# A Strassen pair in a hybrid decoder trunk: the seventh product accumulates in the fifth's PSUM bank, and VectorE instead of GpSimd forms the weight sums

## The chip, the cores and the metric

One NeuronCore of a Trainium2 chip runs the whole program. The metric is the device time of one execution in microseconds (us). Engines: TensorE (PE, with its weight loads as PEld), VectorE (DVE), ScalarE (ACT), GpSimd (POOL), and SyncE (SP), which here only issues DMAs. Each engine works through its own queue in order.

## The reference

The reference is a decoder trunk of two layers over 1024 tokens of width 1024, all in float32. What matters of it:

```
for l in range(DEPTH):                       # DEPTH = 2
    h = rms_norm(x, norm1_w[l]) * (1 + sc1) + sh1
    x = x + g1 * hybrid_mixer(h, w_in[l], w_out[l], ...)
    h = rms_norm(x, norm2_w[l]) * (1 + sc2) + sh2
    x = x + g2 * conv_ffn(h, w_gate[l], w_val[l], conv_w[l], conv_b[l], w_down[l])
return rms_norm(x, final_norm_w)
```

The mixer projects h with one matrix `w_in` into eight groups of 512 columns, runs four retention heads (with a rotary turn of q and k) and four gated-recurrence heads (HGRN2) over them, multiplies by gates and projects back. The FFN forms `silu(conv(h @ w_gate)) * (h @ w_val)` with 2816 columns, then multiplies by `w_down`. The shifts, scales and gates (`sh1` and so on) come from a product with `ada_w`.

## The kernel before, in words

**Split products.** To keep float32 accuracy, every operand is split into a high part (rounded on ACT, line L329 for weights) and the remainder (DVE, L330). A product of a 128-row weight block with 512 tokens is three matmuls: high by high, high by low, low by high (L451, L452, L453). Each matmul has a 128x128 weight and 128x512 moving data.

**Pairs.** Most projections are done two at a time by `pair()`: two blocks of 128 output columns (`g` and `v`), each over all 1024 tokens, form a 2x2 block problem that a Strassen-Winograd scheme solves with seven products instead of eight. The activation side (`b11` to `b22`, and the sums `tops[1]` to `tops[3]`) is prepared once per stage. The weight side is prepared per pair: two DMAs bring `rg` and `rv` (two buffers in all, tag `raw`), four sums of 128x512 are formed on POOL (L472, L473, L474 after the first piece, L476 after the second), and `piece()` splits each of the seven weight blocks, in the order of the products, into six rotating buffers `whi`/`wlo`. `product()` runs 12 matmuls into one bank of a four-bank PSUM pool (tag `pr`). The results are combined by DVE additions that read one operand from SBUF and one from PSUM (`add`, L484); product 1 is copied to SBUF by ACT (L490). In the common order 1, 2, 4, 6, 7, 5, 3 a pair has seven such additions: one each after 2, 6 and 3, two after 7 (the second one uses the bank of product 4, kept until then), and two after 5. A pair with mode "late" (the q/k pair of head 0 in each layer) places product 4 later, because its operand `b12` is ready later; a pair with mode "plain" (the first FFN pair of each layer) uses another order.

**Stages.** In each layer the mixer has 14 pairs (three for f/q, three for the two values, four for q/k, four for the gates), the FFN has 20 (ft = 2 to 21, one of them "plain"). So the program has 68 pairs, 66 of them not "plain". In the mixer the pairs stand between the heads' own work, which generators (`chains`) emit in small steps: `step()` after each product lets every chain emit its next piece. The HGRN chain runs seven levels of small matmuls (L713, L723), each waiting for two DVE multiplications (L731, L732); before them DVE computes the forget gates (L673 to L677). The rotary turn uses a POOL multiplication (L617). In the FFN, `conv_act` runs per pair on ACT and DVE (L955 to L966) and stores through a DMA issued by POOL (L967).

**Other work on DVE.** The product with `ada_w` is done on DVE (L165, L167) in steps that `tick()` emits, one per `step()`. Its raw tiles (`aw`, two buffers) are brought by SP. During the FFN of layer 0 the steps for layer 1 are running; during the FFN of layer 1 there are none.

**Order.** The framework schedules at build time: each engine's order of instructions is fixed before the run, by priority and by a model of when operands are ready. Loads of weights, pieces, weight sums and additions stand in `hp()`, which moves them ahead of everything else by up to 4000 places.

Of the kernel before, what the change touches and what calls it, by code (L numbers as in the profile page):

```python
# [16 lines left out]
P = 128  # L17
# [23 lines left out]
def kernel(  # L41
# [8 lines left out]
    V, A, G, T = nc.vector, nc.scalar, nc.gpsimd, nc.tensor  # L50
# [8 lines left out]
    def hp():  # L59
        return tc.high_priority(offset=ahead[0])  # L60
# [14 lines left out]
    def pr_ps(name):  # L75
        return psum.tile([P, HALF], F32, tag="pr", name=name)
# [249 lines left out]
    def piece(src, n, nm):  # L326
        hi = stg.tile([P, HALF], F32R, tag="whi", bufs=NW, name=f"whi{nm}")
        lo = stg.tile([P, HALF], F32R, tag="wlo", bufs=NW, name=f"wlo{nm}")
        A.activation(hi[:, 0:n], src, AF.Copy)  # L329
        V.tensor_tensor(out=lo[:, 0:n], in0=src, in1=hi[:, 0:n], op=ALU.subtract)  # L330
        return [(hi[:, i:i + P], lo[:, i:i + P]) for i in range(0, n, P)]

    def load_raw(src, n, nm, early=None):
        raw = stg.tile([P, S], F32, tag="raw", bufs=2, name=f"raw{nm}")
        dst = raw[:, 0:n * P].rearrange("p (a b) -> p a b", a=n)
        if early:
            early.dma_start(out=dst, in_=src)
        else:
            with hp(), after_last():
                nc.sync.dma_start(out=dst, in_=src)  # L340
        return raw

    def stage(src, n, nm, early=None):
        raw = load_raw(src, n, nm, early)
        w = []
        with hp():
            for i in range(0, n, 4):
                m = min(4, n - i)
                w += piece(raw[:, i * P:(i + m) * P], m * P, f"{nm}_{i}")
        return w  # L350

    def w_src(w, l, n0, k0=0, n=KT):
        return w[l, k0 * P:(k0 + n) * P, n0:n0 + P].rearrange("(k p) n -> p k n", p=P)
# [23 lines left out]
    def need(n):  # L377
        for _ in range(100):
            if len(zfree) >= n:
                return  # L380
            step()
        raise RuntimeError(f"{len(zfree)} of {n} tiles free")

    def step():
        tick()
        for ch in list(chains):
            ch[0] -= 1
            if ch[0] <= 0:
                ch[0] = next(ch[1], 0)
                if ch[0] == 0:  # L390
                    chains.remove(ch)

    def unit(w, l, n0, nm, wt=None):
        wt = wt or wcols(w, l, n0, nm)
        pss = []
        for half in range(2):
            pss.append(pr_ps(f"u{nm}_{half}"))
            gemm_half(pss[-1], wt, half, range(KT))
            step()
        return pss  # L400
# [41 lines left out]
    def last_operand():  # L442
        for k in range(4):
            split(b12, k, xs[4 + k].t[:, 0:HALF])
            xs[4 + k].free()

    def product(w, b, nm):
        ps = pr_ps(nm)
        for k in range(4):
            (wh, wl), rh, rl = w[k], b[0][:, k, :], b[1][:, k, :]  # L450
            T.matmul(ps, wh, rh, start=k == 0, stop=False)  # L451
            T.matmul(ps, wh, rl, start=False, stop=False)  # L452
            T.matmul(ps, wl, rh, start=False, stop=k == 3)  # L453
        return ps


    ORDERS = {"": (1, 2, 4, 6, 7, 5, 3), "late": (1, 2, 6, 7, 4, 5, 3), "plain": (1, 2, 3, 6, 7, 4, 5)}

    def pair(src_g, src_v, nm, mode=""):
        rg = load_raw(src_g, KT, nm + "g")  # L460
        rv = load_raw(src_v, KT, nm + "v")
        a11, a12, a21, a22 = rg[:, 0:HALF], rg[:, HALF:S], rv[:, 0:HALF], rv[:, HALF:S]
        s1 = stg.tile([P, HALF], F32, tag="s1", bufs=2, name=f"s1{nm}")
        order = ORDERS[mode]
        src = {1: a11, 2: a12, 3: a12, 4: a22, 5: s1, 6: a11, 7: a21}
        right = {1: b11, 2: b21, 3: b22, 4: b12, 5: tops[1], 6: tops[2], 7: tops[3]}
        p = {}
        with hp():
            for i in order:
                p[i] = piece(src[i], HALF, f"{nm}{i}")  # L470
                if i == 1:
                    G.tensor_add(s1, a21, a22)  # L472
                    G.tensor_sub(a21, a11, a21)  # L473
                    G.tensor_sub(a11, s1, a11)  # L474
                elif i == 2:
                    G.tensor_sub(a12, a12, a11)  # L476
        need(2)
        g, v = Z(), Z()
        g0, g1, v0, v1 = g.t[:, 0:HALF], g.t[:, HALF:S], v.t[:, 0:HALF], v.t[:, HALF:S]
        done = {}  # L480

        def add(o, x, y):
            with hp():
                V.tensor_add(o, x, y)  # L484

        for i in order:
            m = done[i] = product(p[i], right[i], f"{nm}_{i}")
            if i == 1:
                with hp():
                    A.activation(v0, m, AF.Copy)  # L490
            elif i == 2:
                add(g0, v0, m)
            elif mode == "plain" and i == 3:
                with hp():
                    A.activation(g1, m, AF.Copy)
            elif i == 3:
                add(g1, g1, m)
            elif mode == "plain" and i == 6:
                add(v0, v0, m)
                with hp():  # L500
                    G.tensor_add(g1, g1, v0)
            elif i == 6:
                add(g1, v0, m)
            elif i == 7:
                add(v1, v0 if mode == "plain" else g1, m)
                if 4 in done:
                    add(v0, v1, done[4])
            elif i == 4 and 7 in done:
                add(v0, v1, m)
            elif i == 5:  # L510
                add(v1, v1, m)
                add(g1, g1, m)
            step()
        return g, v

# [235 lines left out]
    def value_chain(z, box, key, nm):  # L751
        yield 1
        transpose8(z.t, nm, copy_evac)
        yield 1
        box[key] = z

    def run(gen):
        chains.append([next(gen), gen])
# [3 lines left out]
    first, second = TokenNorm(0, 0, 0), TokenNorm(1, 0, 0)  # L762
# [84 lines left out]
    for l in range(DEPTH):  # L847
# [9 lines left out]
        def loose(src):  # L857
            z = Z()
            with hp():
                put(z, src, AF.Copy)  # L860
            return z

        for h in range(HEADS):
            box = {}
            if h:
                ahead[0] = HP
                fsrc, qsrc = pair(w_src(w_in, l, HF + h * P), w_src(w_in, l, HQ + h * P), f"h{l}_{h}")
            else:
                fsrc, qsrc = pre[0], pre[1]
            run(hgrn_chain(l, h, fsrc, qsrc, box))  # L870
            if h:
                a, b = pair(w_src(w_in, l, HV + h * P), w_src(w_in, l, RV + h * P), f"v{l}_{h}")
            else:
                a = loose(pre[2])
                b = loose(unit(w_in, l, RV, f"r{l}_0v", early))
                last_operand()
            if l == 0 and h == 0:
                ada_todo.extend((0, b) for b in range(4, 12))
            run(value_chain(a, box, "h", f"h{l}_{h}v"))
            run(value_chain(b, box, "r", f"r{l}_{h}v"))  # L880
            ahead[0] = HP
            q, k = pair(w_src(w_in, l, h * P), w_src(w_in, l, 512 + h * P), f"r{l}_{h}", "" if h else "late")
            run(ret_chain(l, h, q, k, box))
        m = {}
        order = []
# [32 lines left out]
        def wo_cols(n):  # L918
            w = wcols(w_out, l, n * P, f"wo{l}_{n}")
            return [w[i] for i in order]  # L920
# [3 lines left out]
        for n in range(5):  # L924
            load_xs(n + 1, xd[2 * l])
            w = wo_cols(n)
            for half in range(2):
                ps = pr_ps(f"wo{l}_{n}_{half}")
# [5 lines left out]
        first = TokenNorm(0, l, 1)  # L934
        hooks = {5: {5: first.rstd}, 6: {2: first.turn, 4: first.spread}}
        for half in range(2):
            for n in range(5, KT):
                ps = pr_ps(f"wo{l}_{n}_{half}")
# [34 lines left out]
        for ft in range(PLAIN):  # L973
            nm = f"f{l}_{ft}"
# [44 lines left out]
        for gi, n in enumerate(GROUPS[:-1]):  # L1019
            dw = lambda d: stage(w_src(w_down, l, d * P, starts[gi], n), n, f"dn{l}_{gi}_{d}")  # L1020
            if gi == 0:
                fill(0, 0, 2)
                w = dw(0)
                fill(0, 2, n)
                load_xs(0, xd[2 * l + 1])
            else:
                w = dw(0)
            fill(gi + 1, 0, fresh[gi + 1])
            for d in range(KT):
# [6 lines left out]
                w = dw(d + 1) if d + 1 < KT else None  # L1036
# [4 lines left out]
        nm = f"dn{l}_last"  # L1041
        more = l + 1 < DEPTH
        first, second = TokenNorm(0, l + 1, 0), TokenNorm(1, l + 1, 0)
# [23 lines left out]
        for half in range(2):  # L1067
            sl = slice(half * HALF, (half + 1) * HALF)
            for d in range(KT):
                w = stage(w_src(w_down, l, d * P, f0, GROUPS[-1]), GROUPS[-1], f"{nm}_{d}_{half}")  # L1070
                if half and d in hooks:
                    hooks[d]()
                ps = pr_ps(f"{nm}_{d}_{half}")
# [68 lines left out]
```

## Time and profile before

| | us |
|---|---|
| median of 3 runs | 2635.63 |
| lowest and highest | 2628.96, 2637.62 |
| the profiled execution | 2626.96 |
| its span, first to last instruction | 2625.2 |
| PE busy in the span | 2511.0 (96%) |
| DVE busy | 1873.7 (71%) |
| ACT busy | 998.0 (38%) |
| POOL busy | 603.2 (23%) |
| mean granted TensorE clock | 0.982 of 2.4 GHz |

All rows quoted below come from the profiled execution. Busy shares are averages over stages with different limits, so they are to be read stage by stage. Times inside the trace count from the start of the span. A busy PE is not PE at its peak: matmuls overlap, and one 128x512 matmul starts about 0.23 us after the one before it though each is shown as about 0.39 us long.

### The profile page before, as it was taken

To read this page: it belongs to the slowest core of one execution; us is meant where nothing else is said; L and a number is where in the kernel's file an instruction comes from. 1 tells how busy PE (TensorE), PEld (TensorE's weight loads), DVE (VectorE), ACT (ScalarE), POOL (GpSimd) and SP (SyncE) were. 2 spreads that over 40 slices of the span, in tenths; PEclk is the share of its full clock that TensorE was granted. 3 is DMA by queue.
4 is the path that set the end of the run, shared out by engine and by line. 5 is a ranking of instruction groups with operands and counts; after the bars stand their busy time and mean duration, and the time that the engine had idled before them with its cause. 6 is when DMAs were issued, how large, how long until landed. Compare 5 with 4: busy or idle time off the path is not lost.

```text
span 2625.2 us, 32721 instructions
## 1 busy us (share of the span) xinstructions
PE 2511.0 (96%) x12189; PEld 2069.1 (79%) x12189; DVE 1873.7 (71%) x2781; ACT 998.0 (38%) x1685; POOL 603.2 (23%) x480
## 2 busy tenths in 40 slices
PE   5889999999999999999998999999999999999998
PEld 4777877888788888788877788888877888887887
DVE  7987878865988989744378777777397777774435
ACT  4533433433533333412264334444154333342224
POOL 1512223120423322200013222222133332320000
PEclk7899999999999999999999999999999999999999
DMA  8222313553134444743231112225312222254313
GB/s 294 73 83 86 105 59 95 179 178 93 65 121 135 133 134 147 249 133 95 79 117 57 49 36 70 73 73 154 96 58 78 89 73 88 81 198 139 96 54 107
DMA packets 293920, 283.56 MB, mean 108 GB/s; under 512 B 10793, under 2 KB 240769, under 8 KB 293761
## 3 DMA queue, kind: packets, MB, share of 16 engines
q1 hardware_dynamic: 275904, 219.42, 27.2%
q0 software_dynamic: 17408, 61.88, 6.5%
q8 instruction: 96, 1.57, 0.3%
q14 instruction: 63, 0.52, 0.1%
q10 hardware_dynamic: 449, 0.17, 0.0%
HBM read 229.00 MB, written 52.43 MB: 107 GB/s over the span
## 4 chain that ended last, share of the span: by engine, by line
PE 69%; DVE 8%; issue 5%; DMA 2%; POOL 1%; ACT 1%; POOLq 0%; DVEq 0%; SPq 0%; ACTq 0%
PE f L451 8%; PE f L453 8%; PE f L452 8%; PE dn L529 4%; PE dn L528 4%; PE dn L527 4%; PE wo L527 2%; PE wo L528 2%; PE wo L529 2%; PE dn_last L527 2%; PE dn_last L529 2%; PE dn_last L528 2%; PE g L452 2%; PE g L451 2%; PE g L453 2%
## 5 line engine op out<-in xcount | busy, mean ns | idle before, releaser
L451 PE MATMUL f<-hhi,whif 128*128 128x512 f32 x640 | 253.2, 396 | 3.2 <-DVE z L484 3.2
L453 PE MATMUL f<-hhi,wlof 128*128 128x512 f32 x640 | 251.4, 393 | 0.0
L452 PE MATMUL f<-hlo,whif 128*128 128x512 f32 x640 | 250.0, 391 | 0.0
L484 DVE TENSOR_TENSOR z<-z,f 128x512 f32<-128x512 f32 x278 | 186.3, 682 | 76.9 <-PE f L453 66.8
L451 PE MATMUL f<-thi,whif 128*128 128x512 f32 x480 | 189.8, 395 | 4.4 <-ACT z L490 4.0
L453 PE MATMUL f<-thi,wlof 128*128 128x512 f32 x480 | 189.5, 395 | 0.0
L452 PE MATMUL f<-tlo,whif 128*128 128x512 f32 x480 | 189.5, 395 | 0.0
L529 PE MATMUL dn<-hhi,wlodn 128*128 128x512 f32 x384 | 151.7, 395 | 7.8 <-DVE wlodn L330 7.8
L527 PE MATMUL dn<-hhi,whidn 128*128 128x512 f32 x384 | 150.5, 392 | 0.0
L528 PE MATMUL dn<-hlo,whidn 128*128 128x512 f32 x384 | 150.3, 391 | 0.0
L167 DVE SCALAR_TENSOR_TENSOR ac<-aw,cact,ac 128x512 f32<-128x512 f32 x140 | 125.1, 894 | 30.5 <-DMA aw<-in_ada_w_dram 29.2
L451 PEld LDWEIGHTS f<-hhi,whif 128*128 128x128 f32 x640 | 120.6, 188 | 29.1 <-DVE z L484 2.6
L913 DVE SCALAR_TENSOR_TENSOR z<-dn,mod,z 128x512 f32<-128x512 f32 x64 | 48.0, 749 | 133.2 <-PE dn L529 133.2
L453 PEld LDWEIGHTS f<-hhi,wlof 128*128 128x128 f32 x640 | 120.6, 188 | 27.7
L452 PEld LDWEIGHTS f<-hlo,whif 128*128 128x128 f32 x640 | 120.6, 188 | 26.7
L916 POOL DMA_DIRECT2D xd<-z x48 | 26.0, 541 | 391.2 <-DVE z L913 363.2
L451 PEld LDWEIGHTS f<-thi,whif 128*128 128x128 f32 x480 | 90.6, 189 | 26.9 <-ACT z L490 4.9
L329 ACT ACTIVATE whidn<-rawdn 128x512 fp32r<-128x512 f32 x64 | 39.4, 627 | 184.6 <-PE dn L528 171.0
L453 PEld LDWEIGHTS f<-thi,wlof 128*128 128x128 f32 x480 | 90.5, 188 | 20.9
L452 PEld LDWEIGHTS f<-tlo,whif 128*128 128x128 f32 x480 | 90.3, 188 | 20.8
L713 PEld LDWEIGHTS lh<-z,z 128*128 128x128 f32 x640 | 78.3, 195 | 25.2 <-issue 21.3
L713 PE MATMUL lh<-z,z 128*128 128x64 f32 x640 | 78.5, 276 | 17.8 <-DVE z L732 17.7
(659 smaller groups left out, 6892.7 us busy)
## 6 DMA issues: line engine op xcount, KB each, us to landing
aw<-in_ada_w_dram SPq DMA_DIRECT2D x160, 256.0 KB, 3.0
acts<-z POOLq DMA_DIRECT2D x44, 512.0 KB, 3.0
z<-acts SPq DMA_DIRECT2D x44, 512.0 KB, 4.6
z<-xd POOLq DMA_DIRECT2D x32, 512.0 KB, 5.2
rawdn<-in_w_down_dram SPq DMA_DIRECT2D x32, 512.0 KB, 3.9
xd<-z POOLq DMA_DIRECT2D x52, 256.0 KB, 2.8
rawdn_last<-in_w_down_dram SPq DMA_DIRECT2D x32, 384.0 KB, 3.6
af<-in_ada_w_dram SPq DMA_DIRECT2D x16, 512.0 KB, 10.6
```

The costliest lines, as they stand in the source:

```text
L167: V.scalar_tensor_tensor(out=a, in0=raw, scalar=cact[:, k:k + 1], in1=a, op0=ALU.mult, op1=ALU.add)
L329: A.activation(hi[:, 0:n], src, AF.Copy)
L451: T.matmul(ps, wh, rh, start=k == 0, stop=False)
L452: T.matmul(ps, wh, rl, start=False, stop=False)
L453: T.matmul(ps, wl, rh, start=False, stop=k == 3)
L484: V.tensor_add(o, x, y)
L527: T.matmul(ps, a, rh, start=i == 0, stop=False)
L528: T.matmul(ps, a, rl, start=False, stop=False)
L529: T.matmul(ps, b, rh, start=False, stop=i == last)
L713: T.matmul(ps[:, c * 64:(c + 1) * 64].rearrange("p (b t) -> p b t", t=s), k.t[:, cs], qp.t[:, cs].rearrange("p (b t) -> p b t", t=s)[:, 1: ...
L913: V.scalar_tensor_tensor(out=x, in0=ps, scalar=mod[:, l * 48 + gate + d:][:, 0:1], in1=x, op0=ALU.mult, op1=ALU.add)
L916: nc.gpsimd.dma_start(out=dst[d, :, sl], in_=x)
```

## The change

Four edits to `pair()` and `product()`:

1. The four sums of weights move from POOL (`G`) to DVE (`V`).
2. The order of products becomes 1, 2, 6, 7, 5, 4, 3 for every pair that is not "plain"; the mode "late" goes.
3. Product 3 accumulates onto product 5 in the same PSUM bank, so its first matmul doesn't start a new sum.
4. The additions follow: after 7, `v0 = g1 + m7`; after 5, `v1 = v0 + m5`; after 4, `v0 = v0 + m4`; after 3, `g1 = g1 + (m5 + m3)`. That makes six additions, one fewer. The pair with mode "plain" keeps its additions and order; its sums move to DVE as well.

```diff
-    def product(w, b, nm):
-        ps = pr_ps(nm)
+    def product(w, b, nm, ps=None):
+        first = ps is None
+        ps = pr_ps(nm) if first else ps
...
-            T.matmul(ps, wh, rh, start=k == 0, stop=False)
+            T.matmul(ps, wh, rh, start=first and k == 0, stop=False, skip_group_check=True)
...
-    ORDERS = {"": (1, 2, 4, 6, 7, 5, 3), "late": (1, 2, 6, 7, 4, 5, 3), "plain": (1, 2, 3, 6, 7, 4, 5)}
+    ORDERS = {"": (1, 2, 6, 7, 5, 4, 3), "plain": (1, 2, 3, 6, 7, 4, 5)}
...
                 if i == 1:
-                    G.tensor_add(s1, a21, a22)
-                    G.tensor_sub(a21, a11, a21)
-                    G.tensor_sub(a11, s1, a11)
+                    V.tensor_add(s1, a21, a22)
+                    V.tensor_sub(a21, a11, a21)
+                    V.tensor_sub(a11, s1, a11)
                 elif i == 2:
-                    G.tensor_sub(a12, a12, a11)
+                    V.tensor_sub(a12, a12, a11)
...
-            m = done[i] = product(p[i], right[i], f"{nm}_{i}")
+            m = done[i] = product(p[i], right[i], f"{nm}_{i}", done[5] if i == 3 and not mode else None)
...
             elif i == 7:
-                add(v1, v0 if mode == "plain" else g1, m)
-                if 4 in done:
-                    add(v0, v1, done[4])
-            elif i == 4 and 7 in done:
-                add(v0, v1, m)
+                add(v1 if mode else v0, v0 if mode else g1, m)
+            elif i == 4:
+                add(v0, v1 if mode else v0, m)
             elif i == 5:
-                add(v1, v1, m)
-                add(g1, g1, m)
+                add(v1, v1 if mode else v0, m)
+                if mode:
+                    add(g1, g1, m)
...
-            q, k = pair(w_src(w_in, l, h * P), w_src(w_in, l, 512 + h * P), f"r{l}_{h}", "" if h else "late")
+            q, k = pair(w_src(w_in, l, h * P), w_src(w_in, l, 512 + h * P), f"r{l}_{h}")
```

## Rows read from the trace of the kernel before

**Rows 1.** Page, part 1: busy us, share of span, instructions of PE.

```profile
PE 2511.0 (96%) x12189; PEld 2069.1 (79%) x12189; DVE 1873.7 (71%) x2781; ACT 998.0 (38%) x1685; POOL 603.2 (23%) x480
```

**Rows 2.** Windows: length, busy PE, PEld, DVE, ACT, POOL, clock, DMA share, GB/s.

```profile
103.00:538.00 435.00, 398.62 (x2337) 337.51 (x2338) 355.28 (x597) 163.65 (x342) 114.23 (x73) 0.96 0.33 101
728.60:1086.60 358.00, 357.25 (x1587) 292.64 (x1586) 314.11 (x392) 125.95 (x181) 112.31 (x90) 1.00 0.45 141
1409.70:1811.90 402.20, 380.72 (x2260) 322.98 (x2260) 301.12 (x510) 157.62 (x329) 106.23 (x69) 0.99 0.22 68
2013.60:2304.10 290.50, 290.50 (x1262) 237.01 (x1261) 209.23 (x256) 106.62 (x151) 92.88 (x75) 1.00 0.26 83
```

**Rows 3.** Waits of PE: instruction, for what, us in total, times, longest.

```profile
PE lh L723 <- DVE z L732: 15.9, 7, 3.1
PE v L451 <- ACT z L490: 9.9, 2, 5.8
```

**Rows 4.** Windows of L472, then of L476 (first and last sum): POOL busy, count.

```profile
0.00:2625.20 2625.20, 103.47 (x68) 0.98 0.34 108
...
0.00:2625.20 2625.20, 104.01 (x68) 0.98 0.34 108
```

**Rows 5.** Windows of L330 (first two rows) and of L167 (third): DVE busy, count.

```profile
728.60:1086.60 358.00, 112.92 (x126) 1.00 0.45 141
2013.60:2304.10 290.50, 90.46 (x105) 1.00 0.26 83
...
728.60:1086.60 358.00, 62.59 (x63) 1.00 0.45 141
```

**Rows 6.** Timelines of DVE and SP, one FFN pair of layer 1: start, us, instruction.

```profile
2157.72 1.41 DVE L330 TENSOR_TENSOR wlof<-rawf_12v,whif 128x512 fp32r<-128x512 f32 x1
...
2160.52 0.68 DVE L330 TENSOR_TENSOR wlof<-rawf_12g,whif 128x512 fp32r<-128x512 f32 x1
2161.12 0.68 DVE L484 TENSOR_TENSOR z<-z,f 128x512 f32<-128x512 f32 x1
...
2163.89 0.69 DVE L330 TENSOR_TENSOR wlof<-rawf_12v,whif 128x512 fp32r<-128x512 f32 x1
...
2164.64 0.37 SPq L340 DMA_DIRECT2D rawf_13g<-in_w_gate_dram  x1
```

**Rows 7.** Timelines of PE and DVE, first and last full FFN pair of layer 0.

```profile
737.36 0.40 PE L453 MATMUL f<-thi,wlof 128*128 128x512 f32 x1
740.51 2.06 DVE L484 TENSOR_TENSOR z<-z,f 128x512 f32<-128x512 f32 x3
...
1074.65 0.39 PE L453 MATMUL f<-thi,wlof 128*128 128x512 f32 x1
...
1081.35 0.75 DVE L167 SCALAR_TENSOR_TENSOR ac<-aw,cact,ac 128x512 f32<-128x512 f32 x1 [1.75 <-DMA aw<-in_ada_w_dram]
1082.02 1.28 DVE L484 TENSOR_TENSOR z<-z,f 128x512 f32<-128x512 f32 x2
```

**Rows 8.** Waits of DVE's additions for PE, FFN of layer 0, then of layer 1.

```profile
DVE z L484 <- PE f L453: 2.8, 7, 0.6
...
DVE z L484 <- PE f L453: 55.6, 60, 1.5
```

**Rows 9.** Waits of ACT in the FFN of layer 0: a piece for a sum.

```profile
ACT whif L329 <- POOL rawf_16g L474: 4.0, 1, 4.0
```

**Rows 10.** Timelines of DVE and ACT around the value pair of head 1.

```profile
206.28 0.68 DVE L676 TENSOR_SCALAR z<-z 128x1024 f32<-128x1024 f32 x1
...
1491.41 1.79 DVE L676 TENSOR_SCALAR z<-z 128x1024 f32<-128x1024 f32 x1
...
1494.82 1.76 DVE L330 TENSOR_TENSOR wlor<-rawr_1g,whir 128x512 fp32r<-128x512 f32 x1
...
1499.60 0.60 ACT L490 ACTIVATE z<-v 128x512 f32<-128x512 f32 x1 [4.38 <-DVE z L677]
```

**Rows 11.** Window just after that wait, columns as in rows 2.

```profile
1500.00:1503.50 3.50, 3.25 (x8) 2.60 (x9) 3.50 (x6) 0.20 (x1) 0.00 (x0) 0.55 0.00 0
```

More of the change, by code (lines that the diff above doesn't have):

```diff
@@ L445, in last_operand @@
             xs[4 + k].free()
-    def product(w, b, nm):
-        ps = pr_ps(nm)
+    def product(w, b, nm, ps=None):
+        first = ps is None
+        ps = pr_ps(nm) if first else ps
         for k in range(4):
             (wh, wl), rh, rl = w[k], b[0][:, k, :], b[1][:, k, :]
-            T.matmul(ps, wh, rh, start=k == 0, stop=False)
-            T.matmul(ps, wh, rl, start=False, stop=False)
-            T.matmul(ps, wl, rh, start=False, stop=k == 3)
+            T.matmul(ps, wh, rh, start=first and k == 0, stop=False, skip_group_check=True)
+            T.matmul(ps, wh, rl, start=False, stop=False, skip_group_check=True)
+            T.matmul(ps, wl, rh, start=False, stop=k == 3, skip_group_check=True)
         return ps
-    ORDERS = {"": (1, 2, 4, 6, 7, 5, 3), "late": (1, 2, 6, 7, 4, 5, 3), "plain": (1, 2, 3, 6, 7, 4, 5)}
+    ORDERS = {"": (1, 2, 6, 7, 5, 4, 3), "plain": (1, 2, 3, 6, 7, 4, 5)}
     def pair(src_g, src_v, nm, mode=""):
```

## The prediction, made before the changed kernel was run

> **What bounds the kernel now.** I read the page's first part, then the windows by stage. PE is busy 2511.0 of 2625.2 us [rows 1], so all that any edit can win back is in the other 114 us and in stretches at the lower clock. The windows say where these lie [rows 2]. In the FFN stretch of layer 0, 18 pairs from 728.6 to 1086.6, PE is busy 357.25 of 358 us; in that of layer 1, 15 pairs, 290.50 of 290.50. One pair takes 290.5/15 = 19.37 us there, which is 84 matmuls at 0.23 us. In the two mixers PE is idle 435 - 398.6 = 36.4 and 402.2 - 380.7 = 21.5 us, 58 together; the granted clock is 0.96 and 0.99 there, some 4% of 435 and 1% of 402 or 21 us more. So a gain can come from the mixers alone, at most 58 + 21 = 79 us, and the FFN can only get worse.
>
> Then I read which wait ends last. In the mixers PE waits for DVE: for the level multiplications (L723 on L732, 15.9 us), and twice for the copy of product 1, 5.8 us the longest [rows 3]. So DVE decides, and the change adds to DVE. How full is it? 355 of 435, 314 of 358, 301 of 402 and 209 of 290.5 us [rows 2]: in the FFN of layer 0 a pair has 314/18 = 17.4 us of DVE in 19.9 us, in that of layer 1 13.9 in 19.4.
>
> **The sums on DVE.** The program has 68 x 4 = 272 of them. On DVE two instructions of 128x512 follow each other at 2161.12 - 2160.52 = 0.60 us [rows 6]; I take 0.60 for a sum, because the first of these two has two SBUF inputs as a sum has. That is 4 x 0.60 = 2.4 us a pair. The addition that falls away is worth 0.60, so 1.8 us a pair are added. Against that stands what POOL's sums cost DVE today. They take 103.47/68 = 1.52 us down to the last one's 104.01/68 = 1.53 [rows 4], and while they run, a DVE instruction with both inputs in SBUF is stretched: the remainder L330 takes 0.68 undisturbed and 1.76 beside POOL [rows 6, 10]. In the FFN of layer 0, L330 is 112.92/126 = 0.90 on the mean and L167 62.59/63 = 0.99; with 0.68 and, for L167, 0.75 [rows 7] undisturbed that is 126 x 0.22 + 63 x 0.24 = 43 us in 18 pairs, 2.4 a pair [rows 5]. In layer 1 it is 105 x (90.46/105 - 0.68) = 19 us in 15 pairs, 1.3 a pair [rows 5]. So per pair DVE gains 0.6 us in layer 0 (17.4 to 16.8 of 19.9) and loses 0.5 in layer 1 (13.9 to 14.4 of 19.4). In neither case does it reach PE's time: 0 us, hidden under the products. If the cover were gone, 68 x 1.8 = 122 us would be the price; if all stretching went and no sum found PE waiting, nothing would be lost at all.
>
> The Trainium skill, page "SBUF — State Buffer", section "Who interferes with whom", says that a VectorE instruction with two SBUF inputs contends with a GpSimd instruction that reads SBUF, and that the one that starts second waits until the first has finished. The trace agrees with its direction, 1.76 against 0.68 us [rows 6, 10]. It also speaks against the change: a moved sum has two SBUF inputs itself, and the 16 rotary products stay on POOL, so by the rule a sum that meets one is held as L330 is, 1.08 us, 16 x 1.08 = 17 us of DVE in the mixers at worst. In the FFN the rule leaves the sum as it is.
>
> **What is ready when.** ACT waits up to 4.0 us for POOL's third sum before it can split its block [rows 9]; with sums of 0.60 that wait goes, and ACT is free for its other work. A new wait comes for it: the first sum stands in DVE's in-order queue and needs the second raw block. On POOL it cost nothing to wait. Bounds: 0, if the scheduler has put it behind its DMA's landing, to about 2 us of idle DVE a pair; 16.8 + 2 = 18.8 still fits into 19.9, but additions behind it come later. I take 0.5. The order moves piece 4 (from `rv`) from third to sixth. Today the buffer of `rv` is free after product 7's piece, fifth (2163.89 + 0.69 = 2164.58), and SP issues the next load at once, 2164.64 [rows 6]; it will be one product of 2.75 us later at most. Nothing else is queued on SP behind it in layer 1; in layer 0 the `aw` loads are. Six weight buffers keep the pieces some five products, 13 us, ahead of PE, so this is 0 unless that lead is gone, when it costs its 2.75 us once a pair. POOL's queue loses four sums in front of each store of L967: 0 to a small gain, nobody waits for these stores.
>
> **The shared bank.** Product 3 may start only when `v1 = v0 + m5` has read the bank; between them lies product 4, 12 x 0.23 = 2.75 us. Before, PE hardly waited for any addition in the FFN, its idle time in layer 0's stretch being 358 - 357.25 = 0.75 us in all [rows 2]. In layer 1 the additions come at once: 60 of 105 found DVE idle and waiting for PE. In layer 0 only 7 of 126 did [rows 8], so there additions run late. In the first of its 18 pairs product 5 ends at 737.36 + 0.40 = 737.76, and its addition, the second of three from 740.51, ends about 741.8; product 3 would be due at 740.35: 1.4 us late. In the last it ends at 1082.02 + 0.68 = 1082.7, due 1077.6: 5.1 us late, part of it 1.75 us behind a load of `aw` [rows 7]. Over the 18 pairs these delays add up to some 19 us if nothing else changed. But a stalled PE lets DVE catch up, one addition no longer stands between those of 7 and 5, and DVE has 0.6 us more room a pair and no ACT piece held by POOL. Bounds 0 to 19; I take +4. Layer 1: 0. The accumulation itself costs PE nothing, 12 matmuls as before.
>
> **The mixers.** At the value pair of head 1 product 1's copy waits 4.38 us for the forget-gate chain on DVE, whose instructions are stretched to 1.79 and 1.76 from 0.68 by that pair's neighbour's sums [rows 10]. At least three to four are stretched by 1.1, 3.3 to 4.4 us, and two to four moved sums of 0.60 enter the same chain, 1.2 to 2.4: a gain of 1 to 3 us in each layer, say 4 together, with part of the half-speed window behind it (clock 0.55 over 3.5 us [rows 11]). Elsewhere a block of up to 2.4 us of sums with high priority can come ahead of a level's multiplications in 28 pairs, while POOL's stretching goes: -12 to +12, I take -1. Together -5.
>
> **The sum.** FFN layer 0 +4, FFN layer 1 0, mixers -5: -1 us. The profiled execution took 2626.96 us (span 2625.2), so 2626 there; it lies 8.7 below the median of the runs shown, 2635.63, so I forecast 2634.6 for the median.
>
> **Rivals.**
> - *Faster.* The mixers win more: the chains before L490 and L732 are as relieved as DVE's stretched instructions suggest, and the stalls that let the clock fall become too short for that. For it: PE waits for just these chains [rows 3, 10]. Against: the level waits of L723 lie beside the rotary product, which stays. Price: the 5.8 + 4.1 us at the two L490 waits to a half, 5 us, a quarter of the other 48 us of idle PE, 12, and 3 of the 21 us of clock, with nothing lost in the FFN: -20 us, or 2616.
> - *Slower.* The shared bank: in the FFN of layer 0 the addition of product 5 stays late, and product 3 waits. It decides from where that addition ends over 2.75 us after product 5. For it: 7 of 126 [rows 8] and the two pairs above, whose `aw` waits the change doesn't touch. Against: the relief. Price: 12 of the 19 us, since a stall lets DVE catch up, and 2 for the clock, the mixers unchanged: +14, or 2650.
> - *It does nothing that can be seen.* The sums are formed 13 us ahead of their use, wherever: within a few us of 2635.6. This is the forecast's own side.
>
> **Chances.** A measurement of this kernel can tell some 0.3%, 8 us, from no change. Forecast and third rival, within 8 us: 0.46. Faster, 2608 to 2627: 0.27. Slower, 2644 to 2660: 0.27. The likeliest case has its own range of 2628 to 2643; to leave no more than 2 in 10 out, the range is 2614 to 2654.
>
> **What the next profile would show.** POOL's busy time falls from 603 by about 400 us, DVE's from 1874 moves by no more than 50 either way. L330's mean in both FFN stretches falls to 0.68 to 0.70. The FFN of layer 1 keeps 19.37 us a pair. If the bank is the trouble, PE shows waits of L451 for L484 in the FFN of layer 0. If the sums wait for loads, DVE shows waits for `raw` tiles. I am wrong if the FFN of layer 1 gets slower, or if the mixers move by over 20 us.

## The result, and the profile after

The changed kernel takes 2619.74 us (median of 9 runs, 2616.74 to 2622.28), the kernel before 2633.05 beside it (9 runs, 2624.38 to 2637.62). The ratio is 0.9946, with a 95% interval of 0.9935 to 0.9958: 13 us or 0.5% faster, and more than the 0.3% that a measurement of this kernel can tell. The profiled execution took 2617.09 us, that of before 2626.96. The forecast was 2634.6 within 2614 to 2654, with "faster by over 0.3%" as one of the two less likely cases. So the range held, the middle lay 15 us too high.

In the changed kernel the lines behind L451 stand one lower: matmuls L452 to L454, additions L485, the copy of product 1 L491, the four sums L473, L474, L475, L477. Part 1 of its page, busy us, share and instructions by engine, answers to [rows 1]:

```profile
PE 2515.0 (96%) x12189; PEld 2070.9 (79%) x12189; DVE 1875.5 (72%) x2987; ACT 997.9 (38%) x1685; POOL 201.0 (8%) x208
```

POOL loses 402 us. DVE has 206 instructions more (272 sums come, 66 additions go) and yet only 1.8 us more of busy time: what it took over is paid by what is no longer stretched. That is read off in the windows of L330 and of L167 in the 18 FFN pairs of layer 0, and of L330 in 15 of layer 1 (length, DVE busy and count, clock, DMA share, GB/s), beside [rows 5]:

```profile
717.50:1077.00 359.50, 85.57 (x125) 0.99 0.44 141
2004.00:2294.00 290.00, 71.52 (x105) 1.00 0.25 81
...
717.50:1077.00 359.50, 47.11 (x63) 0.99 0.44 141
```

An L330 now takes 85.57/125 = 0.685 and 71.52/105 = 0.681 us (before 0.90 and 0.86), an L167 47.11/63 = 0.748 (before 0.99). The windows of all engines, in the columns of [rows 2], are these:

```profile
103.00:527.00 424.00, 398.76 (x2332) 338.04 (x2332) 355.74 (x636) 161.03 (x338) 31.88 (x20) 0.96 0.32 104
717.50:1077.00 359.50, 355.70 (x1571) 291.15 (x1570) 302.93 (x445) 129.36 (x183) 9.61 (x18) 0.99 0.44 141
2004.00:2294.00 290.00, 290.00 (x1259) 236.60 (x1258) 214.56 (x300) 106.17 (x150) 7.99 (x15) 1.00 0.25 81
```

In the first the same work has 11 us less, and PE's idle time went from 36.4 to 424 - 398.76 = 25.2 us at the same busy time. In the second PE is idle for 359.5 - 355.7 = 3.8 us, before for 0.75. Where the time went is seen best by the first matmul of each stage in the two traces:

| first matmul of | before, us | after, us | shift |
|---|---|---|---|
| the pairs, layer 0 | 99.71 | 99.32 | -0.4 |
| output projection, layer 0 | 554.51 | 543.07 | -11.5 |
| FFN pairs, layer 0 | 694.90 | 683.29 | -11.6 |
| down projection, layer 0 | 1099.33 | 1089.94 | -9.4 |
| the pairs, layer 1 | 1404.34 | 1395.32 | -9.0 |
| output projection, layer 1 | 1827.97 | 1814.83 | -13.1 |
| FFN pairs, layer 1 | 1968.85 | 1960.86 | -8.0 |
| down projection, layer 1 | 2358.92 | 2348.67 | -10.3 |
| end of the span | 2625.19 | 2615.32 | -9.9 |

The mixer of layer 0 gives 11 us, the FFN of layer 0 takes 2.2 back, the mixer of layer 1 gives 4 and the stage behind it takes 5 back, the FFN of layer 1 gives 2. The waits of PE say which chains were shortened (instruction, what for, us in total, times, longest; beside [rows 3]):

```profile
PE lh L713 <- DVE z L732: 10.6, 5, 4.9
PE v L452 <- ACT z L491: 7.7, 2, 4.3
PE f L452 <- DVE z L485: 6.8, 5, 3.8
...
PE lh L723 <- DVE z L732: 1.9, 1, 1.9
```

The level wait of L723 fell from 15.9 to 1.9 us, that of L713, which was not read for the forecast, from 17.7 to 10.6. The wait for product 1's copy fell only from 9.9 to 7.7. And PE's FFN products now wait 6.8 us for additions, before 3.2. 6.6 of it is in the FFN of layer 0, in four waits. Two of them, 3.80 and 1.30 us, are product 3's and stand between products 4 and 3 of a pair; the other two, 0.97 and 0.50 us, stand before other products and have nothing to do with the shared bank. PE's timeline at the longest, and DVE's below it (start, length, instruction, in brackets the idle time before and what ended it):

```profile
721.60 0.40 PE L454 MATMUL f<-hhi,wlof 128*128 128x512 f32 x1
725.79 0.80 PE L452 MATMUL f<-hhi,whif 128*128 128x512 f32 x1 [3.80 <-DVE z L485]
...
723.85 0.69 DVE L477 TENSOR_TENSOR rawf_4g<-rawf_4g 128x512 f32<-128x512 f32 x1
724.45 0.69 DVE L330 TENSOR_TENSOR wlof<-rawf_4g,whif 128x512 fp32r<-128x512 f32 x1
725.05 0.68 DVE L485 TENSOR_TENSOR z<-z,f 128x512 f32<-128x512 f32 x1
```

Product 3 has to wait until the addition at 725.05 has read product 5's bank; in front of it DVE's queue holds moved sums and the remainders that hang on them. The sums are not all of it: with the sums back on POOL (second experiment) the same product still waits 3.93 us. This is the wait that the prediction named, L452 for L485 in the new numbering.

### The profile page after: what moved, and what is told of

Its sections match the earlier page's. It is cut to its first block, busy times and chain, and to the rows that moved or that the text cites. A ratio compares the mean times of both kernels' runs of the same rounds, so it can differ in the third digit from the quotient of the medians.

```text
span 2615.3 us, 32201 instructions
## 1 busy us (share of the span) xinstructions
PE 2515.0 (96%) x12189; PEld 2070.9 (79%) x12189; DVE 1875.5 (72%) x2987; ACT 997.9 (38%) x1685; POOL 201.0 (8%) x208
## 4 chain that ended last, share of the span: by engine, by line
PE 77%; DVE 13%; DMA 4%; issue 3%; ACT 2%; POOL 0%; SPq 0%; ACTq 0%; DVEq 0%; POOLq 0%
PE f L452 9%; PE f L454 9%; PE f L453 9%; PE dn L529 5%; PE dn L528 4%; PE dn L527 4%; PE lh L713 3%; PE wo L527 2%; PE wo L528 2%; PE wo L529 2%; PE dn_last L527 2%; PE dn_last L529 2%; PE dn_last L528 2%; PE r L452 2%; PE r L454 2%
## 5 line engine op out<-in xcount | busy, mean ns | idle before, releaser
L452 PE MATMUL f<-hhi,whif 128*128 128x512 f32 x640 | 253.8, 397 | 6.8 <-DVE z L485 6.8
L454 PE MATMUL f<-hhi,wlof 128*128 128x512 f32 x640 | 251.6, 393 | 0.0
L485 DVE TENSOR_TENSOR z<-z,f 128x512 f32<-128x512 f32 x240 | 164.1, 685 | 111.4 <-PE f L454 99.3
L452 PE MATMUL f<-thi,whif 128*128 128x512 f32 x480 | 189.5, 395 | 0.2 <-ACT z L607 0.2
L454 PE MATMUL f<-thi,wlof 128*128 128x512 f32 x480 | 189.5, 395 | 0.0
L452 PEld LDWEIGHTS f<-hhi,whif 128*128 128x128 f32 x640 | 120.9, 189 | 33.6 <-DVE z L485 7.2
L454 PEld LDWEIGHTS f<-hhi,wlof 128*128 128x128 f32 x640 | 120.8, 189 | 27.8
L167 DVE SCALAR_TENSOR_TENSOR ac<-aw,cact,ac 128x512 f32<-128x512 f32 x140 | 105.7, 755 | 29.7 <-DMA aw<-in_ada_w_dram 28.3
L452 PEld LDWEIGHTS f<-thi,whif 128*128 128x128 f32 x480 | 90.5, 188 | 21.6 <-ACT z L607 0.6
L454 PEld LDWEIGHTS f<-thi,wlof 128*128 128x128 f32 x480 | 90.5, 188 | 20.9
L713 PEld LDWEIGHTS lh<-z,z 128*128 128x128 f32 x640 | 79.3, 198 | 18.3 <-issue 15.9
L529 PEld LDWEIGHTS dn<-hhi,wlodn 128*128 128x128 f32 x384 | 72.6, 189 | 23.5 <-DVE wlodn L330 7.7
L713 PE MATMUL lh<-z,z 128*128 128x64 f32 x640 | 79.9, 279 | 11.2 <-DVE z L732 10.6
```

Of the source, the lines that this page charges most:

```text
L167: V.scalar_tensor_tensor(out=a, in0=raw, scalar=cact[:, k:k + 1], in1=a, op0=ALU.mult, op1=ALU.add)
L452: T.matmul(ps, wh, rh, start=first and k == 0, stop=False, skip_group_check=True)
L454: T.matmul(ps, wl, rh, start=False, stop=k == 3, skip_group_check=True)
L529: T.matmul(ps, b, rh, start=False, stop=i == last)
L713: T.matmul(ps[:, c * 64:(c + 1) * 64].rearrange("p (b t) -> p b t", t=s), k.t[:, cs], qp.t[:, cs].rearrange("p (b t) -> p b t", t=s)[:, 1: ...
```

## The experiments

They were run in four groups, each beside the kernel before (medians 2632.44, 2633.68, 2635.0 and 2635.8 us). All ratios below are to that kernel, with their 95% intervals.

**The parts of the change.** First the kernel before with the four sums alone moved to DVE.

```diff
-                    G.tensor_add(s1, a21, a22)
+                    V.tensor_add(s1, a21, a22)
... (and so the other three sums)
```

> The kernel before with one edit: the four weight sums of each pair on VectorE; order of products, banks and additions as before. Theory A (the gain comes from VectorE no longer being stretched beside POOL's sums): 8 to 14 us faster than before, nearly all of it in the mixer of layer 0; the mean of L330 in both FFN stretches 0.68 to 0.70 us. Theory B (the gain comes from the new order, the shared bank and the addition saved): within 3 us of before. Theory C (the gain comes from the sums being ready earlier, so that ScalarE isn't held): 8 to 14 us faster, as A.

Measured: 2621.85 us, 0.9955 (0.9937 to 0.9973), 10.6 us faster. L330 falls as in the whole change. So the sums bring 11 of the 13 us, and the order, the shared bank and the saved addition, put together, are worth no more than the rest of 3, which is not told from zero. The total is as theories A and C had it, the place is not. The profiled execution, at 2625.98 us the slowest of the six, has 3.5 us less than before in the mixer of layer 0 (by first matmuls), but 3.7 more in that of layer 1, and the level waits of L723 and L713 fall only from 33.6 to 24.1 us. In which stages the 10.6 us lie is open.

Then the opposite: the whole change, but the four sums stay on POOL.

```diff
-                    V.tensor_add(s1, a21, a22)
+                    G.tensor_add(s1, a21, a22)
... (and so the other three sums)
```

> The changed kernel with the four weight sums back on POOL: new order, shared bank and six additions stay. Theory A: between 2 us faster and 6 us slower than before, and waits of the third product's first matmul for an addition in the FFN of layer 0, since additions run late there; L330 0.86 to 0.90 us. Theory B: 8 to 14 us faster than before. Theory C: as A, but the third product needs POOL's sums earlier, so up to 8 us slower.

Measured: 2670.91 us, 1.0139 (1.0117 to 1.0161), 38 us slower, far outside what was expected: alone, the order with the shared bank is a bad change. PE's longest list of waits now begins with the bank, all of it in the FFN of layer 0:

```profile
PE f L452 <- DVE z L485: 16.2, 14, 3.9
```

12 of these 14 waits, 15.0 us, are product 3's. In the mixers product 3 waits another 14.6 us for additions.

Next the change with product 3 in a bank of its own, and so with the seventh addition.

```diff
-            m = done[i] = product(p[i], right[i], f"{nm}_{i}", done[5] if i == 3 and not mode else None)
+            m = done[i] = product(p[i], right[i], f"{nm}_{i}", None)
...
-                if mode:
-                    add(g1, g1, m)
+                add(g1, g1, m)
```

> The changed kernel with product 3 in a bank of its own again, and so a seventh addition (g1 = g1 + m5); sums on VectorE and the new order stay. Theory A: within 3 us of the changed kernel; the waits of a first matmul for an addition in the FFN of layer 0 (3.8 us the longest) go, VectorE is busy 66 x 0.6 = 40 us more. Theory B: loses 5 us or more against the changed kernel.

Measured: 2613.40 us, 0.9924 (0.9904 to 0.9945), 19 us faster. PE's FFN products wait 1.9 us for additions, the longest 1.1. The saved addition is thus worth less than what the shared bank costs, by some 6 us (0.9946 against 0.9924; the two intervals overlap at their edges), where theory A had no difference and theory B a loss. The FFN of layer 0 takes 398.1 us by first matmuls, with the shared bank 406.7: there the bank costs 8.6 us. From the kernel with the sums alone moved this one differs by the order of products, which here gains some 8 us (0.9955 against 0.9924, again with overlapping edges).

To part order and bank, the last kernel with its sums on POOL, which is the new order alone:

```diff
-                    V.tensor_add(s1, a21, a22)
+                    G.tensor_add(s1, a21, a22)
... (and so the other three sums)
```

> The kernel before with the new order of products alone: sums on POOL, product 3 in a bank of its own, seven additions. It stands beside the run that has the new order and the shared bank with sums on POOL (38 us slower than before). Theory A (those 38 us are the shared bank's, whose release waits for additions that POOL's contention makes late): within 6 us of before, and no wait of PE for an addition in the FFN of layer 0 over 2 us. Rival D (they come from the order: piece 6, third now, needs POOL's third sum): 25 to 40 us slower than before, with PE or ScalarE waiting for pieces.

Measured: 2659.05 us, 1.0088 (1.0069 to 1.0106), 25 us slower. PE's FFN products wait 2.2 us for additions instead of 16.2, so of the 38 us of the run above about 13 belong to the bank and 25 to the order, the lower end of what rival D had. What the order does is seen in ACT: its splits wait for POOL's third sum (here L475), 237 us in 50 cases by these waits, while in the kernel before ACT waits 78 us for POOL's sums. One in the FFN of layer 1, ACT's timeline:

```profile
2108.10 0.63 ACT L329 ACTIVATE whif<-rawf_8g 128x512 fp32r<-128x512 f32 x1 [3.85 <-POOL rawf_8g L475]
```

In the old order the piece for product 4, which needs no sum, stood between the second piece and the one that needs the third sum; in the new one nothing does. The wait alone costs nothing where PE decides: from the first FFN matmul to the down projection's of layer 1 this kernel takes the same time as the one before. Its loss lies in the mixers and at the stages' ends. That ACT's wait for the third sum makes it there is argued, not shown: a kernel in which POOL forms no sums at all, further down, loses as much by this order.

**Contention or latency.** If the gain comes from sums that are sooner ready, POOL work that nobody waits for must be free; if it comes from DVE's stretched instructions, it must cost. So POOL was given additions back whose result nobody reads, in the changed kernel four per pair (`whole[1]` and `whole[2]` are the split blocks of the first two pieces):

```diff
                     V.tensor_sub(a11, s1, a11)
+                    for _ in range(3):
+                        G.tensor_add(junk, whole[1][0], whole[1][1])
                 elif i == 2:
                     V.tensor_sub(a12, a12, a11)
+                    G.tensor_add(junk, whole[2][0], whole[2][1])
```

> The changed kernel with POOL given four additions a pair of the same size that nobody reads, three after the first piece's split and one after the second's: VectorE's sums stay, but POOL reads SBUF beside VectorE as it did before. Theory A: L330 is stretched again to 0.85 us or more in the FFN stretches, and 8 us or more of the gain go, in the mixer of layer 0 above all. Theory B and theory C: within 3 us of the changed kernel, since order, banks and the time at which the sums are ready stay.

Measured: 2780.19 us, 1.0552 (1.0527 to 1.0576), 148 us slower, far more than was expected. The direction speaks for contention, the size says that the test was too coarse: each DVE instruction that overlaps an idle addition, taken against the median of its form elsewhere, adds up to 225 us of stretch, where the real sums in the kernel before make 137; and the shared bank and the idle work together let PE wait 51.7 us for additions. A smaller dose without the shared bank was therefore tried, two idle additions a pair in the kernel with product 3's own bank.

```diff
                     V.tensor_sub(a11, s1, a11)
+                    for _ in range(2):
+                        G.tensor_add(junk, whole[0], whole[1])
```

> Sums on VectorE, new order, product 3 in its own bank (that kernel took 2613 us), and two additions a pair on POOL that nobody reads, after the first piece's split; half of POOL's work before, and no shared bank. Theory A (contention): VectorE busy 80 to 120 us more, and 8 to 30 us slower than without the two additions. Theory C (only the time at which the sums are ready counts): within 4 us of 2613.

Measured: 2659.48 us, 1.0089 (1.0072 to 1.0106), 46 us above the same kernel without them (43 by the two ratios), more than the 30 that theory A had as its most. DVE and POOL in part 1 of its page:

```profile
PE 2528.2 (95%) x12189; PEld 2076.8 (78%) x12189; DVE 2002.3 (75%) x3053; ACT 990.3 (37%) x1685; POOL 413.3 (16%) x344
```

DVE has the same 3053 instructions as without them, and 2002.3 - 1909.2 = 93 us more of busy time. The idle additions share buffers with the real sums and pieces, but no wait in this trace ends with one of them. So POOL's arithmetic costs DVE's time by itself, and the kernel pays for part of it. Whether sums that are ready sooner bring something beside that is not shown by these two runs.

**The rest of POOL's arithmetic.** Then what POOL still computes should go too. The rotary multiplication L617 on DVE, in the kernel with product 3's own bank:

```diff
-        G.tensor_mul(sw.t, sw.t, sn.t)
+        V.tensor_mul(sw.t, sw.t, sn.t)
```

> Sums on VectorE, new order, product 3 in its own bank (2613 us), and the 16 rotary multiplications of 128x1024 on VectorE as well instead of POOL. Theory A: VectorE gets 16 x 1.2 = 19 us more work and loses some 30 us of stretching, level multiplications L731 and L732 fall to 0.68 us; 2 to 8 us faster than 2613, in both mixers. Rival: a rotary multiplication ahead of a level's multiplications in VectorE's queue holds PE, 2 to 8 us slower.

Measured: 2606.63 us, 0.9888 (0.9871 to 0.9906), 7 us better than without it, as theory A had it. But it is not in both mixers: by first matmuls that of layer 0 takes 14.1 us more than without (439.1 to 453.2), that of layer 1 18.5 less (425.4 to 406.9). Then also the sums of the activation side (L419, L431, L436, L438, L439) and the plain pair's two additions (L501 in the kernel before), which leaves POOL without arithmetic:

```diff
-                G.tensor_add(xs[k].t[:, HALF:S], b12[0][:, k, :], b12[1][:, k, :])
+                V.tensor_add(xs[k].t[:, HALF:S], b12[0][:, k, :], b12[1][:, k, :])
...
-            G.tensor_sub(h12, h22, h12)
+            V.tensor_sub(h12, h22, h12)
... (and so L436, L438, L439, L501)
```

> As the one with the rotary multiplications on VectorE, and also the sums of the activation side and the two additions of the plain pairs: POOL has no arithmetic left. Theory A: VectorE gets 38 x 0.6 = 23 us more work and loses some 35 us of stretching at the two stage boundaries of each layer; another 0 to 8 us faster. Rival: at these boundaries two engines shared the work, and one alone takes longer: 4 to 12 us slower than with the rotary multiplications alone.

Measured: 2596.99 us, 0.9850 (0.9829 to 0.9871), another 10 us, a little more than theory A's 8. With all of that moved, the old order and the new one with the shared bank were compared again:

```diff
-        G.tensor_mul(sw.t, sw.t, sn.t)
+        V.tensor_mul(sw.t, sw.t, sn.t)
... (and so every addition, subtraction and multiplication on G)
```

> The kernel before with all of POOL's arithmetic on VectorE; order of products, banks and additions as before. It stands beside the run with the new order, product 3 in its own bank and no arithmetic on POOL (2597 us). Theory A (contention is nearly all of it): within 5 us of 2597. Rival E (the order brings its own part, as the 8 us between the two kernels with the sums alone on VectorE suggest): 5 to 12 us slower than 2597.

> The changed kernel with all of POOL's arithmetic on VectorE; product 3 in the fifth's bank. Theory A (the shared bank costs only where additions run late, and they run late because of contention): within 4 us of 2597. Rival F (the wait for the addition costs whatever the contention, as additions also stand behind loads of the ada product): 4 to 8 us slower than 2597.

Measured: 2572.78 us, 0.9755 (0.9726 to 0.9785), and 2574.38 us, 0.9763 (0.9734 to 0.9792). None of the expectations held: both lie 23 to 24 us below 2597. The first is the kernel before with nothing but the engine changed, and by the two ratios it is some 50 us faster than the changed kernel; part 1 of its page:

```profile
PE 2502.9 (97%) x12189; PEld 2066.3 (80%) x12189; DVE 1883.9 (73%) x3111; ACT 1004.7 (39%) x1685; POOL 79.0 (3%) x150
```

330 instructions have moved to DVE and its busy time grew by 10 us. By first matmuls 15.8 and 15.6 us of the gain lie in the two mixers, 8.1 in the FFN of layer 0, 9.9 in the stage behind that and 6.0 ahead of the first pair. Two causes go together in it: POOL no longer stretches DVE's instructions, and what POOL computed is ready sooner. A rotary multiplication takes 2.71 us on POOL and 1.22 on DVE, and before, ACT waited 18.1 us for POOL's activation sums (L431), of which nothing is left. No run parts the two.

Between these two kernels no difference is left: PE waits for additions 1.9 us in all in the second. So where additions come in time, the shared bank shows no price.

The kernel without POOL arithmetic and with product 3's own bank is 23 us slower than the second of these, though it differs in that bank and one addition. It is also 24 us slower than the first, from which it differs by the order of products alone. With the sums alone moved that order gained 8 us, so what it is worth hangs on the rest of the kernel, and why stays open. Its trace shows more stretches at the lower clock in the mixer of layer 0; the two longest (columns as in [rows 2]):

```profile
144.40:161.50 17.10, 12.95 (x50) 11.75 (x50) 11.38 (x15) 2.71 (x3) 0.00 (x0) 0.50 0.05 15
202.40:212.70 10.30, 8.21 (x32) 7.27 (x31) 8.57 (x13) 1.75 (x4) 0.98 (x1) 0.50 0.13 52
```

To see whether the rotary products hurt there by crowding DVE, those of layer 0 were put back on POOL in this kernel:

```diff
-        V.tensor_mul(sw.t, sw.t, sn.t)
+        (V if l else G).tensor_mul(sw.t, sw.t, sn.t)
```

> As the kernel of 2597 us (new order, own bank), but layer 0's rotary multiplications stay on POOL. In that kernel the mixer of layer 0 lost 12 us against the one with the rotary multiplications on POOL, 17 us of it at half clock behind the level waits. If this is the rotary multiplications' place in VectorE's queue: 4 to 14 us faster than 2597. If it is a shift of the fixed order alone: within 4 us, or slower.

Measured: 2585.66 us, 0.9807 (0.9776 to 0.9837), 11 us faster, as expected of crowding. But the two kernels above have all rotary products on DVE and are faster still. Every one of these kernels also has another fixed order on each engine, and with it other stalls in the mixers; differences of up to some 25 us between kernels that differ in much else are not put down to one mechanism here.

Last, the sums alone on POOL, everything else on DVE, in the old order:

```diff
-                    V.tensor_add(s1, a21, a22)
+                    G.tensor_add(s1, a21, a22)
... (and so the other three sums)
```

> The kernel before with all of POOL's arithmetic on VectorE except the four weight sums of each pair (rotary multiplications, the sums of the activation side and two additions move). Moving the sums alone gave 11 us, moving all 62 us, both with the old order. If the parts add up: 45 to 55 us faster than before. If the sums' contention is what counts wherever they stand (theory A at its plainest, 272 of POOL's 326 arithmetic instructions): at most 20 us faster. In between, each part is worth more when the other has gone.

Measured: 2595.77 us, 0.9856 (0.9831 to 0.9881), between the two expectations. The other 58 instructions (POOL has 208 in the changed kernel and 150 without arithmetic; with the 272 sums that makes 330, not the 326 of the expectation) are so worth 40 us when they move first, while the 272 sums are worth 11 when they move first and 62 - 40 = 22 when they move last (27 by the ratios, over two groups). The sums stretch DVE by 137 us in the kernel before and 149 here, but of the 137 some 70 lie in the pairs of the two FFNs, where PE decides. The 58 stand in the mixers and at the stages' ends, where DVE does; they stretch it by some 65 us before, and some of them are waited for themselves.

## Why the prediction was right, and what was mis-sized

*What bounds the kernel.* Right for the mixers: most of the gain came from there. Not right for the FFN, which "can only get worse" by the forecast: the windows that were read began behind the plain pair of each layer. There PE waited, before the change, 2.0 us in each layer for the copy of product 1, and in layer 0 another 2.17 us for an addition (PE's waits, whole span, columns as in [rows 3]):

```profile
PE f L451 <- ACT z L490: 4.0, 2, 2.0
PE f L451 <- DVE z L484: 3.2, 3, 2.2
```

In the changed kernel the first of these is gone. The FFN of layer 1 gained 2 us by that; in layer 0 the gain is hidden by the bank (below).

*DVE's account.* Right to about a tenth. Per pair 302.93/18 = 16.8 us in layer 0 (forecast 16.8) and 214.56/15 = 14.3 in layer 1 (14.4); L330 and L167 as forecast; POOL -402 (-400). The step that took the stretch from the mean of L330 against its undisturbed length holds. The Trainium skill's page "SBUF — State Buffer", section "Who interferes with whom", says that a VectorE instruction with two SBUF inputs contends with a GpSimd instruction that reads SBUF; the trace agrees in kind, as two idle POOL additions a pair made DVE 93 us busier. What the prediction held against the change by it, sums held by the rotary products for up to 17 us, came to little: the stretch by L617, counted over all DVE instructions, went from some 30 to 34 us.

*The sums' wait for loads.* 0.5 us a pair was taken. DVE waits 22.1 us for `raw` pieces at L473, 0.3 a pair; but 0.5 of it in the FFN of layer 0, none in that of layer 1, and nearly all in the mixers, where DVE has no time to spare. The mean was near, the place was not looked at.

*The value pair of head 1.* A gain of 4 us was forecast, from its chain alone. It mostly did not come: the longest waits for product 1's copy went from 5.8 to 3.3 in layer 0 and from 4.1 to 4.3 in layer 1. DVE's timeline in layer 1, to be held against [rows 10], shows why:

```profile
1476.75 0.69 DVE L473 TENSOR_TENSOR s1r<-rawr_1v 128x512 f32<-128x512 f32 x1 [3.46 <-DMA rawr_1v<-in_w_in_dram]
...
1483.08 0.69 DVE L676 TENSOR_SCALAR z<-z 128x1024 f32<-128x1024 f32 x1
```

The stretch is gone, L676 takes 0.69 instead of 1.79. By this timeline what it gave went into the sums' wait of 3.46 us at the head of the same chain, and into the sums that stand inside it.

*The mixers elsewhere.* This is the mis-sized term: -1 was taken, between -12 and +12. Measured, both mixers give 11 + 4 = 15 us, and with the 2.2 us at the value pairs (9.9 to 7.7) some 13 of that lie elsewhere, 5 of them given back behind the mixer of layer 1. The level waits of L723 and L713 fell by 33.6 - 12.5 = 21 us; in their place others grew, as that of the retention scores for the rotary turn (L639 for L619, 0.2 to 7.0). The end of the bounds was near, the middle was wrong by this reading: the blocks of sums at high priority and the stretching were set off against each other as if alike. But the four sums add 2.4 us to a queue once a pair, while the stretch falls on the multiplications between two levels, for which PE stands waiting. Of the 112 level multiplications (L731, L732) 20 took over 0.8 us before and 4 after, and together they went from 101.0 to 85.1 us. The reading is not shown to the end: with the sums alone moved it is also 4 and 85.2 us, yet that trace keeps 24.1 us of level waits. How much of the 13 us is this relief and how much another fixed order of each engine is open. The "faster" rival named these relieved chains; its 20 us were too many, since the clock of the first window stayed at 0.96 and the waits behind the levels grew.

*The shared bank.* The place and the mechanism were right; that the stage came out near the term, +2.2 for +4, is luck. Against the kernel with product 3's own bank the bank costs 8.6 us in the FFN of layer 0 (398.1 to 406.7 by first matmuls), over twice the term: 5.1 us of waits of product 3, the longest 3.8, and a stretch at the lower clock behind that one (the stage's mean granted clock is 0.99 with it and 1.00 without). What hid this are 6.3 us that the same stage gains without the shared bank, 404.4 before to 398.1, which the forecast had at nothing. The reason for relief was right: 37 of some 108 additions (six a pair) now find DVE idle and waiting for PE, before 7 of 126 [rows 8]. The "slower" rival holds where that relief is taken away: with the sums left on POOL the FFN of layer 0 takes 423.8 us, and 405.3 with the same order and product 3's own bank, so the bank costs 18.5 there; 14 had been given, with 19 as the bound. So what decides on its price is how late the additions run, and that hangs on POOL.

*The order.* It was costed at nothing, for the buffer of `rv` alone. By itself it costs 25 us with the sums on POOL, gains some 8 with the sums alone on DVE, and costs 24 again with no arithmetic on POOL. That the third sum is needed one piece sooner fits the first of these figures and can't explain the last. In the change the sums are on DVE, so the total did not show it.

*The sum.* -1 was forecast, -10 measured between the two profiled executions (2626.96 to 2617.09): -15 in the mixers for -5, +2 for +4, and +3 for 0 in the rest, the +5 behind the mixer of layer 1 and the -2 in its FFN. The direction of each large term was right; that the total stayed within the range owes something to the bank's price, which took back part of what the mixers and the FFN gained beyond the forecast.

## What to carry to other kernels

Read a helper engine's arithmetic by what it does to the engine beside it: divide the mean of an instruction by its undisturbed length, stage by stage, and price the difference where that engine decides, not on the mean. Let the window of a stage begin with its first matmul: here two waits that the change removed lay just ahead of the windows. Before a sum is moved off POOL, look at all else that POOL computes; here 58 instructions in the mixers and at the stages' ends were worth more than 272 sums. Take a change of order as having no fixed worth: the same one gained 8 us in one kernel and lost 24 in another. A bank that is used again before it is read needs additions in time; measure how many of them come late before counting the addition that is saved.

## What the runs showed of the hardware that was not expected

- POOL's work was not free though nobody waited for it. Two additions a pair, 136 of 1.5 us or some 210 us of POOL, made DVE 93 us busier at the same number of instructions, and the kernel 43 to 46 us longer.
- After the one wait of 3.80 us in the FFN, the granted clock was 0.50 until 729, the lower of its two levels, 0.78 on the mean of the next 4 us, and 1.00 from 733. By these rows the stall cost 3.3 x 0.50 + 4 x 0.22 = 2.5 us beside its own length. Windows from 725.7, columns as above:

```profile
725.70:729.00 3.30, 3.21 (x8) 2.54 (x9) 1.84 (x4) 0.00 (x0) 0.00 (x0) 0.50 0.01 2
729.00:733.00 4.00, 4.00 (x15) 3.21 (x14) 1.29 (x2) 1.77 (x2) 0.00 (x0) 0.78 0.00 0
733.00:737.00 4.00, 4.00 (x19) 3.28 (x18) 3.42 (x4) 1.85 (x4) 0.00 (x0) 1.00 0.58 167
```
